# The first mixer of a two-layer decoder trunk, put in another order: keys first, one substitution for four groups, output projection in parts

## The chip, the cores and the metric

The kernel runs on one core of one Trainium2 chip. The metric is the time that the device takes for one execution of the whole program, in microseconds. Three runs of the kernel before took 2907.27, 2908.19 and 2913.11 us; their median, 2908.19 us, is the time that the change is compared with. The changed kernel computes the same function of the same inputs.

## The reference

The program is a trunk of two layers over 256 tokens of width 2048, in float32. Layer 0 mixes tokens with a gated DeltaNet, layer 1 with a sparse attention; each layer then has a normalization, a gated feed-forward part (5120 wide), another normalization and a gated addition. Only the mixer of layer 0 and the projection behind it are touched:

```python
def gdn_mixer(x, w_in, conv_w, a_log, dt_bias, norm_g, w_o):
    proj = x @ w_in                                   # 2048 x 12352
    qkv, z, a, b = ...
    qkv = silu(causal_dwconv(qkv, conv_w))            # four taps
    q, k = l2norm(q) * 128 ** -0.5, l2norm(k)         # 16 heads of 128
    beta, g = sigmoid(b), -exp(a_log) * softplus(a + dt_bias)   # 32 heads
    o = gated_delta_rule(q, k, v, g, beta)            # v: 32 heads of 128
    o = o * rsqrt(mean(o * o) + eps) * norm_g * silu(z)
    return o @ w_o                                    # 4096 x 2048
...
x = layer_norm(DN_ALPHA * x + gdn_mixer(x, ...), ln1_g[0], ln1_b[0])
```

Inside the delta rule a unit lower triangular system is solved for every head and chunk of tokens: (I + L) u = rhs, where L holds products of keys, scaled by beta and by decays exp(gc_i - gc_j). The kernel works with two chunks of 128 tokens, not four of 64, which gives the same result.

## The kernel before

**Large products.** Every product with weights is done in pieces of 512 KB (128 x 1024 numbers). `weights()` loads a piece on SP's queue into `raw` (three buffers), ScalarE copies it to `hi` in a shorter format (L107), and VectorE writes the rest to `lo` (L108), three buffers each; both have the priority of instructions 1000 places earlier. TensorE then multiplies hi with both halves of x and lo with one. `gemm_t_steps` does it with the weights as the stationary side (8 matmuls of 512 columns and 8 of 256 for one piece, output in PSUM tiles `mm_ps`), `gemm_steps` with x as the stationary side (12 matmuls of 512 columns, or 24 of 256, output `b_ps`). Both draw their PSUM tiles from the same ring "mm" of four banks, two at a time.

**Groups.** The mixer treats the 16 key heads and 32 value heads in eight groups g of two key heads and four value heads. For a group it runs, in the order of the program:

- `values(g)`: v, 8 pieces with four tiles of 128 columns, each convolved by `conv` (`fold` copies half of the PSUM tile on ScalarE, L186, VectorE adds the other half into `pd`, L187, then `ac` and three taps, tanh and a product), transposed and scaled into `vt`
- `zgate(g)`: the gate z, 8 pieces
- `keys(g+1)`: k and q of the next group, 4 pieces each, convolved in the same way
- `inverses(g)`: GpSimd loads the inverses of the 32 x 32 diagonal blocks into `pm`, TensorE multiplies them with L (`w_ps`), ScalarE copies that into W
- `front(g+1)`: decays from the rows `grow` (loaded by SP into `qd`), sums of squares, the products of keys and queries (`g_ps`), L; then L goes to DRAM (`lt`) and comes back as `ld` in another layout, and GpSimd inverts the diagonal blocks by 31 steps of a multiplication (L505) and a subtraction (L507), eight columns wide, masks L, and sends the inverses to DRAM (`tt`)
- `solve(g)`: for both chunks a (0 and 1) the start y0 = pm rhs, then three times y = y0 - W y, the last of which is u; each step is four small matmuls into `s_ps` (L517) and a subtraction on VectorE (L567). Between the chunks `rhs` gets the part of u of chunk 0 (`vt`, L559), and y0 is copied on ScalarE (L562)
- `outputs(g)`: o for both chunks (`o_ps`), its squares on ScalarE (`sqs`, L582, a ring of its own), rsqrt on VectorE, the product with z (`ot`), a transposition and the split into `oT`.

**What sets the order.** The engines run their instructions in order. The order on each is decided by a scheduler when the program is built: among the instructions whose inputs and buffers are there by its own estimate, it takes the one that stands first in the program. A tile of a ring can be written when the earlier users of its buffer are through. So large products of later groups can be drawn in between the steps of a solve, as long as buffers for them are free.

**Behind the groups.** `oT` holds all 32 heads. `project()` multiplies them with w_o in five blocks of columns (three of 512, two of 256, 64 pieces), adds them to x, which is loaded a second time (L870), takes the statistics, and `layer_norm` follows.

The lines that matter most here:

```python
def fold(self, pool, out, ps):
    t = pool.tile([P, S], F32, tag="fold", name="fold", bufs=2)
    nc.scalar.activation(t[:m], ps[:, S:], AF.Copy)
    nc.vector.tensor_tensor(out, ps[:, :S], t[:m], op=ALU.add)
...
sq = pool.tile([P, P], F32, tag="sqs", name="sqs")
for h in h4:
    nc.scalar.activation(sq, ps[:, h], AF.Square, accum_out=...)
```

## Time and profile before

The profile is one execution, taken by the hardware profiler; times inside it count from the start of its span.

| | |
|---|---|
| median of three runs | 2908.19 us (2907.27 to 2913.11) |
| span of the profiled execution, which is also its time here | 2914.3 us |
| the mixer's groups (first large matmul to the last `oT`) | 12.8 to 869 us |
| its output projection (`b_ps<-hi,oT`) | 757.7 to 970 us |
| substitution on GpSimd (L505, L507) | 496 operations, 229.9 us busy |
| VectorE, first 970 us | 662.0 us busy |
| ScalarE, first 970 us | 454.3 us busy |
| TensorE, first 970 us | 903.7 us busy |

An engine's busy time is the time in which an instruction of it was running; a pause is printed in brackets with what ended it. TensorE is the engine with the least slack, so what counts is what it waits for and at which clock it runs (1.00 is full speed, 0.50 half). Other engines' pauses cost nothing as long as TensorE does not wait for them.

### The profile page before, as it was taken

What the parts mean: (1) busy time and instruction counts of PE and PEld (TensorE: products, weight loads), DVE (VectorE), ACT (ScalarE), POOL (GpSimd) and SP (SyncE); (2) the same over time, 40 slices, a digit from 0 to 9 for tenths busy, and PEclk for the clock granted to TensorE, in tenths of its full rate; (3) what the DMA queues carried; (4) which work ended last, traced back from release to release, by engine and by line L of the source; (5) the groups of instructions that cost most, each with busy time, mean ns of one, the idle gap of its engine ahead of it and who ended that gap; (6) DMA issues with size and microseconds to landing.
All of it is one profiled execution on the core that took longest, in us unless ns stands there. A gap on an engine that the chain in (4) does not pass through costs nothing.

```text
span 2914.3 us, 41870 instructions
## 1 busy us (share of the span) xinstructions
PE 2826.4 (97%) x15790; PEld 2458.8 (84%) x15790; DVE 1860.0 (64%) x3148; ACT 1399.7 (48%) x2147; POOL 399.3 (14%) x720
## 2 busy tenths in 40 slices
PE   8899999999899999999999999999999999999999
PEld 7677888788688888888888988888888888888887
DVE  6667876787455666666545575666566666654465
ACT  4444554455333555555433453455465555543344
POOL 0552445344400000000000000030000000000000
PEclk9999999999999999999999999999999999999999
DMA  7655555556456566667655566554556666665555
GB/s 196 165 127 136 158 157 154 150 150 164 119 184 205 160 200 201 205 201 206 195 194 195 173 200 196 169 178 145 184 168 195 195 189 195 196 194 193 190 181 188
DMA packets 425947, 520.94 MB, mean 179 GB/s; under 512 B 28268, under 2 KB 329712, under 8 KB 425488
## 3 DMA queue, kind: packets, MB, share of 16 engines
q1 hardware_dynamic: 418576, 499.91, 56.6%
q0 software_dynamic: 7168, 18.35, 2.6%
q8 instruction: 124, 2.03, 0.3%
q14 instruction: 79, 0.65, 0.1%
HBM read 513.94 MB, written 7.39 MB: 179 GB/s over the span
## 4 chain that ended last, share of the span: by engine, by line
PE 83%; DMA 7%; DVE 4%; POOL 2%; issue 2%; ACT 2%; SPq 0%; DVEq 0%; ACTq 0%; POOLq 0%
PE mm_ps L126 31%; PE mm_ps L130 16%; PE b_ps L150 10%; PE b_ps L154 10%; PE b_ps L151 10%; DMA raw<-in_gdn_w_in 2%; DVE lo L108 2%; PE s_ps L517 2%; POOL xt L505 1%; DMA qd<-grow 1%; POOL xi L507 1%; ACT hi L107 1%; DMA raw<-in_ple_w_gate 1%; DMA ld<-lt 1%; PE w_ps L517 1%
## 5 line engine op out<-in xcount | busy, mean ns | idle before, releaser
L108 DVE TENSOR_TENSOR lo<-raw,hi 128x1024 fp32r<-128x1024 f32 x925 | 1135.5, 1229 | 878.1 <-ACT hi L107 841.6
L107 ACT ACTIVATE hi<-raw 128x1024 fp32r<-128x1024 f32 x925 | 977.0, 1057 | 1268.5 <-PE b_ps L151 489.3
L126 PE MATMUL mm_ps<-xT,hi 128*128 128x512 f32 x4176 | 1072.1, 396 | 19.2 <-DVE pd L187 6.8
L126 PEld LDWEIGHTS mm_ps<-xT,hi 128*128 128x128 f32 x4176 | 752.2, 190 | 154.1 <-ACT hi L107 12.5
L130 PEld LDWEIGHTS mm_ps<-xT,lo 128*128 128x128 f32 x4176 | 578.5, 190 | 43.6
L130 PE MATMUL mm_ps<-xT,lo 128*128 128x256 f32 x4176 | 602.2, 284 | 0.0
L150 PE MATMUL b_ps<-hi,xT 128*128 128x512 f32 (+2 forms) x736 | 277.9, 385 | 9.9 <-ACT hi L107 8.9
L151 PE MATMUL b_ps<-hi,xT 128*128 128x512 f32 (+2 forms) x736 | 276.0, 381 | 0.0
L151 PE MATMUL b_ps<-hi,hTA 128*128 128x512 f32 (+1 forms) x640 | 212.2, 347 | 0.0
L150 PE MATMUL b_ps<-hi,hTA 128*128 128x512 f32 (+1 forms) x640 | 212.2, 347 | 0.0
L154 PE MATMUL b_ps<-lo,xT 128*128 128x512 f32 (+2 forms) x736 | 190.5, 380 | 1.5 <-DVE lo L108 1.5
L150 PEld LDWEIGHTS b_ps<-hi,xT 128*128 128x128 f32 x736 | 140.7, 191 | 37.4 <-ACT hi L107 11.5
L203 POOL DMA_DIRECT2D lng<-in_ln_g x16 | 9.4, 589 | 1145.3 <-DVE lo L108 560.8
L151 PEld LDWEIGHTS b_ps<-hi,xT 128*128 128x128 f32 x736 | 139.8, 190 | 24.0 <-DVE xT L291 0.3
L154 PEld LDWEIGHTS b_ps<-lo,xT 128*128 128x128 f32 x736 | 132.8, 190 | 26.6 <-DVE lo L108 1.9
L154 PE MATMUL b_ps<-lo,hTA 128*128 128x512 f32 (+1 forms) x640 | 138.6, 347 | 0.0
L151 PEld LDWEIGHTS b_ps<-hi,hTA 128*128 128x128 f32 x640 | 121.2, 189 | 15.0
L150 PEld LDWEIGHTS b_ps<-hi,hTA 128*128 128x128 f32 x640 | 121.2, 189 | 15.0
L505 POOL TENSOR_TENSOR xt<-ld,xi 128x60 f32<-128x60 f32 (+24 forms) x248 | 113.5, 458 | 89.7 <-DMA ld<-lt 70.9
L507 POOL TENSOR_TENSOR xi<-xi,xt 128x60 f32<-128x60 f32 (+24 forms) x248 | 116.4, 469 | 19.4
L154 PEld LDWEIGHTS b_ps<-lo,hTA 128*128 128x128 f32 x640 | 105.1, 189 | 15.0
L150 PE MATMUL b_ps<-hi,oT 128*128 128x512 f32 (+1 forms) x320 | 108.0, 353 | 0.6 <-DVE x L225 0.5
(260 smaller groups left out, 2637.0 us busy)
## 6 DMA issues: line engine op xcount, KB each, us to landing
raw<-in_gdn_w_in SPq DMA_DIRECT2D x193, 512.0 KB, 4.3
raw<-in_ffn_w_gate SPq DMA_DIRECT2D x160, 512.0 KB, 5.0
raw<-in_ffn_w_up SPq DMA_DIRECT2D x160, 512.0 KB, 4.7
raw<-in_ffn_w_down SPq DMA_DIRECT2D x160, 512.0 KB, 3.5
raw<-in_dsa_w_in SPq DMA_DIRECT2D x80, 512.0 KB, 3.6
raw<-in_gdn_w_o SPq DMA_DIRECT2D x64, 512.0 KB, 3.7
raw<-in_ple_w_gate SPq DMA_DIRECT2D x64, 512.0 KB, 3.9
raw<-in_dsa_w_o SPq DMA_DIRECT2D x32, 512.0 KB, 4.0
```

The lines of the kernel that those rows point to most:

```text
L107: nc.scalar.activation(hi, raw, AF.Copy)
L108: ins = nc.vector.tensor_tensor(lo, raw, hi.bitcast(F32), op=ALU.subtract)
L126: nc.tensor.matmul(q[:m, :], hi[:, k, o:o + m], x[:, k0 + k].rearrange("p a b -> p (a b)"), start=k0 + k == 0, stop=False)
L130: nc.tensor.matmul(q[:m, S:], lo[:, k, o:o + m], x[:, k0 + k, 0, :], start=False, stop=k0 + k == kt - 1)
L150: nc.tensor.matmul(ps[a][:, :n], xh, hi[:, k, :], start=k0 + k == 0, stop=False)
L151: nc.tensor.matmul(ps[a][:, :n], xl, hi[:, k, :], start=False, stop=False)
L154: self.last = nc.tensor.matmul(ps[a][:, :n], x(k0 + k)[:, 0, a * P:(a + 1) * P], lo[:, k, :], start=False, stop=k0 + k == kt - 1)
L203: ins = self.nc.gpsimd.dma_start(out=r, in_=bass.AP(tensor=src.tensor, offset=src.offset, ap=[[0, P], [1, n]]))
L505: nc.gpsimd.tensor_tensor(tmp[:, :m, :w], bcast(ld[:, i + 1:, i], m, 1), xi[:, :m, i:i + 1].to_broadcast([P, m, w]), op=ALU.mult)
L507: nc.gpsimd.tensor_tensor(xi[:, :m, i + 1:], xi[:, :m, i + 1:], tmp[:, :m, :w], op=ALU.subtract)
L517: nc.tensor.matmul(ps[:, h], lhs[:, h], rhs[:, h], start=first, stop=last)
```

## The change

- **Keys.** The keys of groups 0 to 3 are computed first, those of 4 to 7 behind the first group's values and gate. All eight stay in SBUF. Queries are computed group by group (`queries(g+1)`).
- **Substitution.** `lower(g)` makes L of a group and sends its diagonal blocks to DRAM on GpSimd's queue. `substitution()` loads those of four groups as `ld`, one 32 x 32 block on each of the 128 partitions, turns the blocks over into `lT`, and runs the 31 steps on VectorE: one multiplication and one subtraction each, over all columns done so far. It is a generator: `weights()` takes `share` steps out of it with every piece of weights, two for the first four groups and one for the second, and what is left is drained in one go (the line `self.go_(self.aside)`).
- **Masks and clamps.** The mask on L is multiplied in where W is written, now on VectorE, and the mask on q k^T on two products instead of four. The clamps of the decays go from VectorE to ScalarE (Relu with a bias), and `lower` and `front` both load the rows of `grow`.
- **Outputs.** Both chunks share one rsqrt of 8 columns. The scratch of the squares is a tile of the ring "fold". `oT` is a tile of one group, in a ring of two.
- **Projection in parts.** `mixed(g, n)` multiplies the heads of n groups with their rows of w_o in four blocks of 512 columns and adds the product to x, which stays where it was loaded first: two groups at a time, ahead of the solves of groups 2, 4 and 6, and group 6 alone behind the solve of group 7. `project()` has the four heads of group 7 left.

The first two fences are TensorE's order at the end of group 1's solve: `s_ps` are the steps of the solve, `o_ps` its output products, `mm_ps` large matmuls (of values of group 2). Before:

```order
L517 MATMUL s_ps<-y,W 128x128 x4
L126 MATMUL mm_ps<-xT,hi 128x512 x7
L130 MATMUL mm_ps<-xT,lo 128x256 x8
L126 MATMUL mm_ps<-xT,hi 128x512 x8
L130 MATMUL mm_ps<-xT,lo 128x256
L517 MATMUL s_ps<-y,W 128x128 x4
L579 MATMUL o_ps<-u,qd 128x128 x4
L130 MATMUL mm_ps<-xT,lo 128x256 x7
L126 MATMUL mm_ps<-xT,hi 128x512 x8
```

and of the change, where line numbers are its own:

```order
L504 MATMUL s_ps<-y,W 128x128 x4
L124 MATMUL mm_ps<-xT,hi 128x512 x3
L128 MATMUL mm_ps<-xT,lo 128x256 x8
L504 MATMUL s_ps<-y,W 128x128 x4
L504 MATMUL s_ps<-u,n_2186 128x128 x4
L504 MATMUL s_ps<-vt,pm 128x128 x4
L504 MATMUL s_ps<-y_2919,W 128x128 x4
L504 MATMUL s_ps<-y,W 128x128 x8
L608 MATMUL o_ps<-u,qd 128x128 x4
L607 MATMUL o_ps<-u,qo 128x128
L608 MATMUL o_ps<-u,qd 128x128
```

What moved: before, every step of the solve is followed by large matmuls; in the change the last six steps and the output products stand one behind the other, without a large matmul between them.

The second place is ScalarE's order around the squares of a group (`sqs`), with the `fold` of the convolutions that follow. Before, at group 3:

```order
L562 ACTIVATE y_4341<-s_ps 128x512
L540 ACTIVATE vt<-v_ps,sv 128x128 x8
L107 ACTIVATE hi<-raw 128x1024 x5
L582 ACTIVATE sqs,oss<-o_ps 128x128 x4
L107 ACTIVATE hi<-raw 128x1024 x2
L186 ACTIVATE fold<-mm_ps 128x256 x2
L402 ACTIVATE ac<-pd_110,cw 128x256
```

and in the change, at group 1:

```order
L590 ACTIVATE y_2919<-s_ps 128x512
L611 ACTIVATE sqs,oss<-o_ps 128x128 x5
L184 ACTIVATE fold<-mm_ps 128x256
L611 ACTIVATE sqs,oss<-o_ps 128x128 x3
L406 ACTIVATE ac<-pd_109,cw 128x256
L184 ACTIVATE fold<-mm_ps 128x256 x2
L468 ACTIVATE L<-qd,ngc 128x128 x8
```

What moved: the folds of the next group's values now stand behind the squares whose buffers they take over, the first one behind the four squares of chunk 0 (and one of chunk 1), the second behind those of chunk 1, and between y0 and the squares no `hi` is left. Behind them come the clamps of `lower`, eight in a row.

The third place is VectorE's order in the solve of group 3, where the substitution of the second four groups is drained (`xt` and `xi` are its two operations). Before, the steps y, y and u of chunk 1, at group 1:

```order
L567 TENSOR_TENSOR y<-y_2447,s_ps 128x512
L108 TENSOR_TENSOR lo<-raw,hi 128x1024 x2
L567 TENSOR_TENSOR y<-y_2447,s_ps 128x512
L108 TENSOR_TENSOR lo<-raw,hi 128x1024
L567 TENSOR_TENSOR u<-y_2447,s_ps 128x512
```

and in the change, the end of 33 operations of the substitution in a row:

```order
L497 TENSOR_TENSOR xi<-xi,xt 128x26x6
L495 TENSOR_TENSOR xt<-lT,xi 128x135
L497 TENSOR_TENSOR xi<-xi,xt 128x27x5
L495 TENSOR_TENSOR xt<-lT,xi 128x112
L497 TENSOR_TENSOR xi<-xi,xt 128x28x4
L495 TENSOR_TENSOR xt<-lT,xi 128x87
L497 TENSOR_TENSOR xi<-xi,xt 128x29x3
L495 TENSOR_TENSOR xt<-lT,xi 128x60
L497 TENSOR_TENSOR xi<-xi,xt 128x30x2
L495 TENSOR_TENSOR xt<-lT,xi 128x31
L595 TENSOR_TENSOR u<-y_4753,s_ps 128x512
```

What moved: the substitution, which stood on GpSimd, is on VectorE ahead of a step of the solve. The diff, cut to its core:

```diff
@@ weights()
+        for _ in range(self.share):
+            next(self.aside, None)
         return hi, lo
@@ residual()
-    def residual(self, xb, ps, st):
-        self.nc.vector.scalar_tensor_tensor(xb, xb, ALPHA, ps, op0=ALU.mult, op1=ALU.add)
-        self.nc.vector.bn_stats(st, xb)
+    def residual(self, xb, ps, st, scale=ALPHA):
+        if scale == 1.0:
+            self.nc.vector.tensor_tensor(xb, xb, ps, op=ALU.add)
+        else:
+            self.nc.vector.scalar_tensor_tensor(xb, xb, scale, ps, op0=ALU.mult, op1=ALU.add)
+        if st is not None:
+            self.nc.vector.bn_stats(st, xb)
@@ gdn_groups()
+        def lower(g, s):
+            i, k = g % 4, ks[g]
+            dm = rows_of(g)
+            L = Ls[g] = pool.tile([P, 2, 4, P], F32, tag="L", name="L", bufs=6)
...
+            for a in range(2):
+                for h in h4:
+                    nc.scalar.activation(L[:, a, h], dm[:, a, h], AF.Relu,
+                                         bias=self.ngc[:, a, 4 * g + h:4 * g + h + 1])
+                nc.scalar.activation(L[:, a], L[:, a], AF.Exp, scale=-1.0)
...
+            for b in range(4):
+                nc.gpsimd.dma_start(out=s["lt"][i, :, b].rearrange("q i j -> i q j"),
+                                    in_=L[32 * b:32 * b + 32, :, :, 32 * b:32 * b + 32].rearrange("p a h j -> p (a h) j"))
+
+        def substitution(s):
+            lt, tt = s["lt"], s["tt"]
+            ld = pool.tile([P, 32, 32], F32, tag="zs", name="ld")
+            nc.gpsimd.dma_start(out=ld, in_=lt.rearrange("g q b i j -> (g q b) i j"))
+            lT = pool.tile([P, 32, 32], F32, tag="u", name="lT")
+            nc.vector.tensor_copy(lT, ld.rearrange("p i j -> p j i"))
...
             for i in range(31):
-                w, m = 31 - i, i // 4 + 1
-                nc.gpsimd.tensor_tensor(tmp[:, :m, :w], bcast(ld[:, i + 1:, i], m, 1),
+                m, w = i + 1, 31 - i
+                tmp = pool.tile([P, 256], F32, tag="xt", name="xt")
+                tv = tmp[:, :m * w].rearrange("p (c j) -> p c j", c=m)
+                nc.vector.tensor_tensor(tv, bcast(lT[:, i, i + 1:], m, 1),
                                         xi[:, :m, i:i + 1].to_broadcast([P, m, w]), op=ALU.mult)
-                nc.gpsimd.tensor_tensor(xi[:, :m, i + 1:], xi[:, :m, i + 1:], tmp[:, :m, :w], op=ALU.subtract)
+                nc.vector.tensor_tensor(xi[:, :m, i + 1:], xi[:, :m, i + 1:], tv, op=ALU.subtract)
+                yield
@@ outputs()
-                sq = pool.tile([P, P], F32, tag="sqs", name="sqs")
+                sq = pool.tile([P, S], F32, tag="fold", name="sqs", bufs=2)[:, :P]
                 for h in h4:
                     nc.scalar.activation(sq, ps[:, h], AF.Square, accum_out=ss[:, a, h // 2, h % 2:h % 2 + 1])
...
+        def mixed(g, n):
+            scale = ALPHA if not g else 1.0
+            h = lambda k: self.heads[g + k // 4][:, k % 4]
+            for nb in range(4):
+                c = nb * 512
+                self.gemm(t["gdn_w_o"][4 * g * P:], c, 512, h, 4 * n,
+                          lambda a, ps: self.residual(self.x[:, a, c:c + 512], ps, None, scale))
...
+        b0 = scales(0)
+        for g in range(4):
+            lower(g, b0)
+        n = queries(0)
+        self.aside, self.share = substitution(b0), 2
+        f = front(0, n)
+        vt, zs = values(0, b0), zgate(0)
+        self.go_(self.aside)
+        self.share = 0
+        for g in range(4, 8):
+            self.go_(key_steps(g))
+        b1 = scales(1)
         for g in range(8):
-            s = n
-            values(s)
-            zgate(s)
-            if g < 7:
-                n = keys(g + 1)
-            inverses(s)
-            if g < 7:
-                front(n)
-            solve(s)
-            outputs(s)
+            s = b1 if g > 3 else b0
+            if g:
+                vt, zs = values(g, s), zgate(g)
+            n = queries(g + 1) if g < 7 else None
+            if g == 4:
+                self.go_(self.aside)
+                self.share = 0
+            inverses(g, s)
+            if g < 7:
+                e = front(g + 1, n)
+            if g in (2, 4, 6):
+                mixed(g - 2, 2)
+            u = solve(g, s, f, vt)
+            if g == 7:
+                mixed(6, 1)
+            outputs(g, f, u, zs)
+            f = e
+            if g == 1:
+                lower(4, b1)
+                lower(5, b1)
+            if g == 2:
+                lower(6, b1)
+                lower(7, b1)
+                self.aside, self.share = substitution(b1), 1
@@ run()
-        x = self.x = xp.tile([P, 2, D], F32, tag="x", name="x")
-        nc.sync.dma_start(out=x, in_=t["x"].rearrange("(a q) d -> q a d", q=P))
...
-            affine = self.project(pool, t["gdn_w_o"], lambda k: oT[:, k], 32, t["ln1_g"][0], t["ln1_b"][0],
-                                  lambda: self.prepare(0, pp), side=2)
+            affine = self.project(pool, t["gdn_w_o"][28 * P:], lambda k: last[:, k], 4, t["ln1_g"][0], t["ln1_b"][0],
+                                  lambda: self.prepare(0, pp), side=2, scale=1.0)
```

More of the change, by code (lines that the diff above doesn't have):

```diff
@@ L88, in __init__ @@
         self.behind = []
+        self.aside, self.share = iter(()), 0
+        self.xp = pool(name="xp", bufs=1, side="right")
+        self.x = self.xp.tile([P, 2, D], F32, tag="x", name="x")
     def after(self, ins, to, sync=False):
@@ L429, in keys @@
-        def keys(g):
-            s = {"g": g}
-            q = s["q"] = pool.tile([P, 2, S], F32, tag="q", name="q")
-            k = s["k"] = pool.tile([P, 2, S], F32, tag="k", name="k")
-            steps = (self.gemm_t_steps(w_in, 2048 + 256 * g, 256, self.xT, conv(16 + 2 * g, lambda n: k[:, n])),
-                     self.gemm_t_steps(w_in, 256 * g, 256, self.xT, conv(2 * g, lambda n: q[:, n])))
-            if not g:
-                for nb in range(4):
-                    load(nb)
-                    next(steps[0])
-                gates()
-            for x in steps:
-                self.go_(x)
-            return s
@@ L444, in sums @@
[L444 to L458 removed]
+        ks = {}
@@ new lines, in key_steps, with squares @@
+        def key_steps(g):
+            k = ks[g] = pool.tile([P, 2, S], F32, tag="k", name="k", bufs=8)
+            return self.gemm_t_steps(w_in, 2048 + 256 * g, 256, self.xT, conv(16 + 2 * g, lambda n: k[:, n]))
+        def squares(y, ps):
+            sq = pool.tile([P, 2, S], F32, tag="y0", name="sq")
+            nc.scalar.activation(sq, y, AF.Square)
+            for h in range(2):
+                for a in range(2):
+                    nc.tensor.matmul(ps[:, 2 * h + a:][:, 0:1], sq[:, h, a * P:(a + 1) * P],
+                                     self.ones[:, 0:1], start=True, stop=True)
@@ L459, in sums, with scales @@
+        def scales(b):
+            pss = self.sp.tile([P, 16], F32, tag="sp", name="kk_ps")
+            for i in range(4):
+                squares(ks[4 * b + i], pss[:, 4 * i:4 * i + 4])
+            ss, ik = small("kss", 16), small("kik", 16)
+            c, nc1, sv = small("c", 2, 8, 2), small("nc1", 16), small("sv", 2, 8, 2)
             nc.vector.tensor_scalar(ss, pss, 4 * RMS_EPS, None, op0=ALU.add)
-            rk = self.rsqrt(pool, ss[:, 0:4], 4)
+            rk = self.rsqrt(pool, ss, 16)
@@ L515, in mul, with inverses @@
+                yield
+            nc.gpsimd.dma_start(out=tt.rearrange("g q b c j -> (g q b) c j"), in_=xi)
+        def mul(lhs, rhs, ps=None):
             ps = ps if ps is not None else self.sp.tile([P, 4, P], F32, tag="bk", name="s_ps")
             for h in h4:
-                nc.tensor.matmul(ps[:, h], lhs[:, h], rhs[:, h], start=first, stop=last)
+                nc.tensor.matmul(ps[:, h], lhs[:, h], rhs[:, h], start=True, stop=True)
             return ps
-        def inverses(s):
+        def inverses(g, s):
@@ L618, in project @@
-    def project(self, pool, src, h, kt, g, b, prepare, side=1):
+        def mixed(g, n):
[5 more added lines that the diff above has]
+                          lambda a, ps: self.residual(self.x[:, a, c:c + 512], ps, None, scale))
+        first = [key_steps(g) for g in (0, 1)]
+        for nb in range(4):
+            load(nb)
+            for x in first:
+                next(x)
@@ L619, in project @@
+    def project(self, pool, src, h, kt, g, b, prepare, side=1, scale=ALPHA):
         blocks = ((0, 512), (512, 512), (1024, 512), (1536, 256), (1792, 256))
```

234 lines of the change are left out of this document (114 added, 120 removed).

## The prediction

> **What bounds the kernel now.** The page comes first. TensorE is busy for 97% of the span, and the change touches only the first mixer, so the question is where TensorE stands still or runs slowly there, and whether the new order makes that less or more.
>
> ```profile
> span 2914.3 us, 41870 instructions
> PE 2826.4 (97%) x15790; PEld 2458.8 (84%) x15790; DVE 1860.0 (64%) x3148; ACT 1399.7 (48%) x2147; POOL 399.3 (14%) x720
> ```
>
> The busy time by stretches of the mixer is the second view. The columns are the stretch, its length, the busy time of PE, its weight loads, DVE, ACT and POOL (with counts), the granted clock, the DMA share and GB/s. Group 0 is begun before 150 us, the last group's solve falls after 750 us, and the output projection ends near 970 us.
>
> ```profile
> 50.00:150.00 100.00, 83.50 (x448) 71.45 (x447) 68.78 (x141) 45.16 (x78) 42.84 (x76) 0.94 0.62 165
> 150.00:750.00 600.00, 570.90 (x3316) 497.29 (x3316) 454.14 (x1039) 303.30 (x575) 258.14 (x472) 0.98 0.56 150
> 750.00:800.00 50.00, 41.38 (x202) 35.09 (x201) 23.47 (x52) 17.76 (x39) 24.16 (x52) 0.86 0.35 104
> 800.00:970.00 170.00, 169.40 (x969) 148.23 (x968) 89.73 (x122) 65.71 (x77) 5.36 (x12) 1.00 0.60 193
> ```
>
> From 50 to 150 us TensorE idles 16.5 us, over the 600 us of the steady groups 29.1 us, from 750 to 800 us 8.6 us, and then hardly at all. That is all the idle time that a better order can give back, some 54 us, with the slow clock that follows long pauses (0.94, 0.98 and 0.86). The timeline of TensorE names the two large pauses of the first group and shows what a pause costs afterwards.
>
> ```profile
> 106.48 3.66 PE L126 MATMUL mm_ps<-xT,hi 128*128 128x512 f32 x8 [5.73 <-ACT hi L107]
> 109.98 1.11 PE L130 MATMUL mm_ps<-xT,lo 128*128 128x256 f32 x8
> 110.93 2.00 PE L126 MATMUL mm_ps<-xT,hi 128*128 128x512 f32 x8
> 148.68 1.57 PE L517 MATMUL w_ps<-pm,L 128*128 128x96 f32 x6 [9.29 <-DMA pm<-tt]
> ```
>
> The first 8 matmuls after the pause of 5.73 us take 109.98 - 106.48 = 3.5 us, the next 8 (110.93 on) 2.00: 1.5 us are lost to the slow clock. The 9.29 us are the wait for the inverses that GpSimd works out one group at a time.
>
> **What the change takes away.** (1) The two pauses of group 0, 15.0 us, and about 4.5 us of slow clock behind them (1.5 as above, twice that for the longer pause): 19.5 us. Their cause goes, since the substitution of four groups now has the matmuls of keys 4 to 7, 16 pieces of weights, as cover. (2) The pauses from 750 to 800 us: 8.6 us, and 4.4 for the clock, which is 0.14 below full over 50 us but partly in the pauses themselves: 13 us. (3) Of the 29.1 us of the steady groups about half, 14.5, since some end on weights that queue on SP behind the transfers of L and ld (these move to GpSimd's queue), others on the convolution, which stays; with half of the clock loss (0.02 of 600 us) 6 us: 20 us. (4) In the projection 14 pieces of 256 columns become pieces of 512. The starts of the lo matmuls that close two successive pieces of 512 columns tell what one takes:
>
> ```profile
> 1501.88 1.07 PE L154 MATMUL b_ps<-lo,hTA 128*128 128x512 f32 x4
> 1504.60 1.07 PE L154 MATMUL b_ps<-lo,hTA 128*128 128x512 f32 x4
> 1600.06 1.12 PE L154 MATMUL b_ps<-lo,hTA 128*128 128x256 f32 x8
> 1602.93 1.12 PE L154 MATMUL b_ps<-lo,hTA 128*128 128x256 f32 x8
> ```
>
> 2.72 against 2.87 us, so 14 x 0.15 = 2.1 us. Sum taken away: 54.6 us; 36 if the steady pauses all stay, 76 if they all go with their clock loss (41 in place of 20).
>
> **What it adds: seven open tails.** The order shows the price. In outputs() the scratch of the squares is now taken from the ring "fold" of two buffers, out of which every convolution's first step also draws. So the folds of values(g+1) wait for the squares of group g, the four PSUM tiles of the large matmuls stay full, and TensorE has nothing to put between the last steps of solve(g): in the rows above, s_ps, s_ps, s_ps, o_ps stand one behind the other, where before some twenty large matmuls stood between two steps. The length of a step is read where VectorE was waiting for it (timeline of all engines):
>
> ```profile
> 840.52 1.05 PE L517 MATMUL s_ps<-y,W 128*128 128x128 f32 x8
> 841.41 1.06 PE L579 MATMUL o_ps<-u,qd 128*128 128x128 f32 x8
> 841.62 0.69 DVE L567 TENSOR_TENSOR u<-y,s_ps 128x512 f32<-128x512 f32 x1 [1.30 <-PE s_ps L517]
> 842.51 0.28 ACT L582 ACTIVATE sqs<-o_ps 128x128 f32<-128x128 f32 x1 [0.73 <-PE o_ps L579]
> 842.91 0.28 ACT L582 ACTIVATE sqs<-o_ps 128x128 f32<-128x128 f32 x1
> ```
>
> VectorE begins 1.10 us after the step's first matmul (841.62 - 840.52) and needs 0.69. How soon TensorE follows, a place shows where it waited for vt:
>
> ```profile
> 651.12 1.11 DVE L559 SCALAR_TENSOR_TENSOR vt<-s_ps,nc,vt 128x128 f32<-128x128 f32 x4
> 651.52 0.75 PE L517 MATMUL s_ps<-vt,pm 128*128 128x128 f32 x4 [0.61 <-DVE vt L559]
> ```
>
> The first of the four vt (336 ns, below) ends at 651.46, and TensorE starts 0.06 later. A step is 1.85 us. TensorE is taken for 0.81 of it (a little less than 841.41 - 840.52), so each step leaves 1.04 us idle. The rest of the tail comes from the groups by line:
>
> ```profile
> L559 DVE SCALAR_TENSOR_TENSOR vt<-s_ps,nc,vt 128x128 f32<-128x128 f32 x32 | 8.9, 336 | 0.0
> L562 ACT ACTIVATE y<-s_ps 128x512 f32<-128x512 f32 x16 | 9.4, 587 | 4.1 <-PE s_ps L517 3.7 <-PE ss_ps L453 0.4
> L186 ACT ACTIVATE fold<-mm_ps 128x256 f32<-128x256 f32 x64 | 20.8, 373 | 1.1 <-PE mm_ps L130 0.7
> L187 DVE TENSOR_TENSOR pd<-mm_ps,fold 128x256 f32<-128x256 f32 x64 | 24.1, 413 | 0.0
> L402 ACT ACTIVATE ac<-pd,cw 128x256 f32<-128x256 f32 x64 | 29.4, 501 | 21.2 <-DVE pd L187 20.6
> ```
>
> In groups 0, 1, 3 and 5, which have no projection in between: four steps that end in y or u, 4.2 us; the step through vt, which TensorE follows head by head, 1.2; y0 on ScalarE (0.59, and the drain of its matmuls) 0.9. Then the 12 output matmuls of the two halves take about 2.5 us (24 records at 0.1), while five squares at 0.40 (842.91 - 842.51) from 1.10 on end at 3.1, a fold (0.37) and its add (0.41) at 3.95: 1.45 idle. Two large matmuls later the second bank is wanted, which waits for three squares, ac (0.50), fold and add: 2.5 less 0.45, 2.0. Sum 9.75 us. In groups 2, 4 and 6 the projection of two groups fills the first half and three steps stay open: 3.1 + 0.3 + 3.45 = 6.9. Together 4 x 9.75 + 3 x 6.9 = 60 us; 45 if each hand-over costs nothing.
>
> In a tail TensorE works about 45% of the time. What the clock makes of that is read at a like place:
>
> ```profile
> 238.12 1.11 PE L477 MATMUL g_ps<-k 128*128 128x256 f32 x4
> 240.88 0.30 PE L592 MATMUL ot_ps<-ident,ot 128*128 128x128 f32 x1 [1.65 <-DVE ot L588]
> 242.18 0.84 PE L592 MATMUL ot_ps<-ident,ot 128*128 128x128 f32 x3 [1.00 <-DVE ot L588]
> 242.91 1.92 PE L517 MATMUL w_ps<-pm,L 128*128 128x96 f32 x8
> 250.60 1.03 PE L517 MATMUL w_ps<-pm,L 128*128 128x96 f32 x8
> 238.00:244.00 6.00, 3.35 (x17) 2.45 (x16) 5.56 (x15) 3.91 (x10) 0.00 (x0) 0.92 0.52 144
> 244.00:246.00 2.00, 2.00 (x8) 1.71 (x8) 2.00 (x5) 1.51 (x4) 0.00 (x0) 0.50 0.53 184
> 374.00:380.00 6.00, 3.38 (x19) 2.31 (x17) 6.00 (x14) 3.20 (x6) 5.06 (x13) 1.00 0.31 87
> 380.00:382.00 2.00, 1.96 (x11) 1.50 (x10) 2.00 (x3) 2.00 (x7) 1.84 (x3) 1.00 0.82 208
> ```
>
> Pauses of 1.65 and 1.00 us, with TensorE busy 3.35 of 6 us, were enough for the same 8 matmuls to take 1.92 us in place of 1.03, with 0.50 of the clock granted; a stretch as thin at 374 us (3.38 of 6) kept the full clock. A tail at half clock throughout its second half would lose about 5 us, with 1.7 us on the large matmuls behind it nearly 7, one untouched nothing. The two places tie, so I take 2.5 for each tail, 17.5 us, and keep 0 and 49 as ends. The Trainium skill, "TensorE: Matmul & The Clock Gate" (section "Why this matters for your kernels"), advises pauses of no more than about 3 us if the clock is to hold; by that rule the 17.5 would be 0 and the sum smaller by as much. The trace agrees at 374 us and not at 244, where pauses of at most 1.65 us stood ahead of a clock of 0.50.
>
> **Three smaller terms.** The substitution on VectorE is 31 steps of two operations for four groups. A 128x256 add takes 0.413 us (L187) and, from the next row, a 128x512 one 0.681, so 1.05 ns an element and 0.145 fixed.
>
> ```profile
> L567 DVE TENSOR_TENSOR y<-y,s_ps 128x512 f32<-128x512 f32 x32 | 21.8, 681 | 11.6 <-PE s_ps L517 11.6
> L505 POOL TENSOR_TENSOR xt<-ld,xi 128x60 f32<-128x60 f32 (+24 forms) x248 | 113.5, 458 | 89.7 <-DMA ld<-lt 70.9
> L247 DVE TENSOR_TENSOR rt<-rs 128x4 f32<-128x4 f32 x72 | 13.2, 184 | 1.4
> L419 ACT ACTIVATE qo<-qd,go 128x128 f32<-128x128 f32 x32 | 10.3, 391 | 22.1 <-DMA qd<-grow 22.1
> ```
>
> A set has 2 x 5456 elements (the sum over the steps of columns done by columns left): 11.4 + 62 x 0.145 = 20.4 us, two sets 41 us, against 230 us in 496 operations (L505 and its twin) on GpSimd, which nothing but group 0 and the last group waited for. VectorE was busy 454 of 600 us, so there is room, except at one place: the rest of the second set is drained ahead of group 4, and in VectorE's order 33 of its operations with some 6190 elements stand between y and u of group 3, without a lo among them. That is 6.5 + 4.8 = 11.3 us in front of a step that TensorE waits for; less what the step has already been charged, 9.5 us. Second, group 7: its solve is covered by the projection of group 6 up to u of the first half, but vt, y0, three steps, the squares, twelve small operations of rsqrt (0.18 each, L247), ot and oT stand ahead of the last projection: 1.2 + 0.9 + 3.1, then about 7 after the output matmuls, and 3 for the clock: 15 us (9 to 20). Third, ScalarE gets the clamps that VectorE did: 128 activations at about 0.39 (L419 is the like form), 50 us, of which lower() and front() put some 20 in a row ahead of hi in three places. The three pieces of weights that are split ahead cover about 8 us; I charge 6 us (0 to 25).
>
> The other moves I cost at nothing: masks on VectorE (16 adds of 256 and 16 of 384 elements), the smaller rsqrt count, 32 more adds into x at 0.68, since VectorE's sum stays within 10 us of what it was; x is loaded once, not twice (2 MB less), and the rows of grow twice (4 MB more). Without that slack these would show as TensorE waiting for lo.
>
> **Sum.** Added: 60 + 17.5 + 9.5 + 15 + 6 = 108; taken away 55; net +53. The profiled span of 2914.3 lies 6.1 above the median of the three runs, so 2914.3 + 53 - 6.1 = 2961 us. Low end: added 45 + 0 + 8 + 9 + 0 = 62, taken away 76: 2894. High end: 60 + 49 + 11 + 20 + 25 = 165, taken away 36: 3037.
>
> **Rivals.** (A) Faster: the wait for the inverses and SP's crowded queue were the real cost, and the tails are cheap. With 76 taken away and 8 + 9 added for the drain and group 7, the seven tails must cost less than 59 us, 8.4 each, to come out ahead; at 45 the time is 2894. For it: the 9.29 and 5.73 us pauses are real and do go. Against it: the step of 1.85 us is measured, and the order leaves no large matmul in the tails. (B) The clock stays whole, because no single pause in a tail is much longer than 2 us: 2961 - 17.5 = 2943. The row at 380 us is for it, the row at 244 us against it. (C) The clock falls to half in every tail: 2961 + 31.5 = 2992; the same two rows, the other way round. B is also what the Trainium skill's rule on pauses gives. (D) The bursts on ScalarE and VectorE are not covered, so that TensorE waits for hi and lo after each tail as well: 2961 + 19 = 2980, and with C 3011.
>
> **How the numbers follow.** Something near the forecast, tails at 60 with some of the clock, 0.45; B 0.15; C and D together 0.23; A 0.12, ending below 2902; the rest, 0.05, lands within 0.2% of the time before (about what a measurement of this kernel can tell from no change). So slower 0.83, same 0.05, faster 0.12. The range runs from A's side to C with D, 2898 to 3020.
>
> **What would show it.** In the profile of the changed kernel each of groups 0 to 6 should show TensorE waiting for VectorE's y and u, some 1 us each, four or three times, with a granted clock under 0.9 there, and a wait of the first z matmuls for pd; the wait of w_ps for pm and the pauses from 100 to 150 us should be gone; group 3 should have one pause of about 10 us. I am wrong if the tails together idle under 45 us, or if a large matmul stands between their steps.

## The result, and the profile after

The changed kernel takes 2934.22 us (median of 5 runs, 2921.75 to 2939.18), the kernel before, timed beside it, 2909.56 us (2907.27 to 2913.49). The ratio is 1.0075 with a 95% interval of 1.0056 to 1.0094: slower by 22 us by the ratio, 18.1 by the profiled spans. The forecast was 2961, slower by 53 us; the direction and the range hold, the size is more than twice too large.

The page, as for the kernel before:

```profile
span 2932.4 us, 40943 instructions
PE 2835.6 (97%) x15654; PEld 2462.2 (84%) x15654; DVE 1854.8 (63%) x3007; ACT 1426.5 (49%) x2259; POOL 115.3 (4%) x192
```

GpSimd gave up 284 us of work and VectorE is no busier, yet the span is 18.1 us longer. The busy time by stretches (length, PE, weight loads, DVE, ACT, POOL, granted clock, DMA share, GB/s) shows where; the mixer now ends at 992.9 us, where the first transposition of the normalization starts, before at 976.1:

```profile
50.00:150.00 100.00, 94.91 (x525) 82.00 (x524) 80.09 (x188) 69.11 (x148) 11.54 (x20) 0.97 0.68 190
150.00:500.00 350.00, 333.55 (x1880) 288.63 (x1880) 237.65 (x463) 178.69 (x350) 20.71 (x36) 0.99 0.54 155
500.00:600.00 100.00, 77.63 (x416) 67.73 (x415) 72.17 (x160) 41.08 (x86) 2.91 (x5) 0.85 0.39 122
600.00:900.00 300.00, 288.76 (x1577) 248.87 (x1576) 186.67 (x309) 138.95 (x248) 6.92 (x12) 0.99 0.51 153
900.00:992.90 92.90, 84.48 (x437) 71.69 (x436) 62.12 (x124) 35.28 (x59) 5.31 (x12) 0.93 0.41 134
```

The first group's pauses went (95 of 100 us busy, 83.5 before). One stretch stands out: 500 to 600 us, 22 us idle at a clock of 0.85. What TensorE waited for from 150 to 900 us, by the view of waits (instruction, what it waited for, us in all, times, longest), is a list of the tails and little else:

```profile
PE s_ps L504 <- DVE u L595: 17.8, 4, 14.3
PE s_ps L504 <- DVE y L595: 11.4, 14, 0.9
PE b_ps L148 <- DVE pd L185: 8.3, 7, 1.2
PE mm_ps L124 <- DVE pd L185: 4.1, 1, 4.1
PE s_ps L504 <- ACT y L590: 3.5, 7, 0.7
PE s_ps L504 <- DVE vt L587: 1.8, 4, 0.4
```

Without the one wait of 14.3 us for u, the waits of the seven tails add up to 3.5 + 11.4 + 8.3 + 3.5 + 1.8 = 28.5 us idle. The same view of the kernel before, 150 to 800 us, names quite other things:

```profile
PE ot_ps L592 <- DVE ot L588: 10.5, 5, 4.6
PE b_ps L150 <- ACT hi L107: 8.3, 4, 3.3
PE mm_ps L126 <- DVE pd L187: 6.8, 3, 3.0
PE v_ps L538 <- DVE v L407: 6.4, 5, 2.7
PE s_ps L517 <- DVE vt L559: 3.5, 3, 1.8
```

One tail in full, TensorE's timeline of the changed kernel at the end of group 1 (start, length, matmuls, and in brackets the idle time before and what ended it):

```profile
320.15 1.05 PE L504 MATMUL s_ps<-y,W 128*128 128x128 f32 x8
322.37 1.16 PE L504 MATMUL s_ps<-u,n 128*128 128x128 f32 x8 [1.16 <-DVE u L595]
323.97 1.26 PE L504 MATMUL s_ps<-vt,pm 128*128 128x128 f32 x8 [0.45 <-DVE vt L587]
325.92 1.16 PE L504 MATMUL s_ps<-y,W 128*128 128x128 f32 x8 [0.69 <-ACT y L590]
327.93 1.16 PE L504 MATMUL s_ps<-y,W 128*128 128x128 f32 x8 [0.85 <-DVE y L595]
329.87 1.64 PE L504 MATMUL s_ps<-y,W 128*128 128x128 f32 x8 [0.78 <-DVE y L595]
331.30 1.91 PE L608 MATMUL o_ps<-u,qd 128*128 128x128 f32 x8
333.00 0.63 PE L607 MATMUL o_ps<-u,qo 128*128 128x128 f32 x2
...
334.95 0.39 PE L608 MATMUL o_ps<-u,qd 128*128 128x128 f32 x2
336.52 0.50 PE L148 MATMUL b_ps<-hi,xT 128*128 128x512 f32 x1 [1.19 <-DVE pd L185]
```

From 320.15 to 336.52 are 16.37 us for 72 small matmuls, which follow each other every 0.111 us where nothing delays them: 8.0. So the tail costs 8.4 us (8.5 with the first gate matmul, as the table has it). Counted in this way (starts of rows, less 0.111 us for a small matmul, 0.119 for one of 256 columns, 0.227 for one of 512), all of the mixer gives this account of lost time:

| lost time, us | before | after |
|---|---|---|
| to 50 us | 10.8 | 12.3 |
| 50 to 150 us | 20.9 | 5.2, and 4.6 in one wait ahead of the first gate matmul |
| tails of groups 0 to 6 | | 9.7, 8.5, 4.3, 10.8, 4.3, 8.2, 4.3 = 50.1 |
| wait for u in group 3 | | 14.6 |
| end of group 7 | in the next row | 14.9 |
| all else (before: to 750, to 800, to 976 us) | 52.7 + 14.5 + 2.7 = 69.9 | 17.7 |
| sum to the normalization | 101.6 | 119.4 |

### The profile page after: what moved, and what is told of

It reads as the page before. It is cut to its first block, busy times and chain, and to the rows that moved or that the text cites. A ratio compares the mean times of both kernels' runs of the same rounds, so it can differ in the third digit from the quotient of the medians.

```text
span 2932.4 us, 40943 instructions
## 1 busy us (share of the span) xinstructions
PE 2835.6 (97%) x15654; PEld 2462.2 (84%) x15654; DVE 1854.8 (63%) x3007; ACT 1426.5 (49%) x2259; POOL 115.3 (4%) x192
## 4 chain that ended last, share of the span: by engine, by line
PE 91%; issue 3%; ACT 2%; DVE 2%; DMA 1%; POOL 0%; DVEq 0%; SPq 0%; ACTq 0%; POOLq 0%
PE mm_ps L124 31%; PE mm_ps L128 16%; PE b_ps L148 13%; PE b_ps L149 13%; PE b_ps L152 12%; PE s_ps L504 3%; PE o_ps L608 1%; ACT hi L103 1%; DMA qd<-grow 1%; DVE lo L104 0%; PE w_ps L504 0%; DVE y L595 0%; PE lg_ps L910 0%; PE sc_ps L860 0%; PE ot_ps L624 0%
## 5 line engine op out<-in xcount | busy, mean ns | idle before, releaser
L124 PE MATMUL mm_ps<-xT,hi 128*128 128x512 f32 (+1 forms) x4176 | 1068.2, 396 | 15.2 <-DVE mv L235 4.6
L124 PEld LDWEIGHTS mm_ps<-xT,hi 128*128 128x128 f32 (+1 forms) x4176 | 752.2, 190 | 150.2 <-ACT hi L103 9.2
L128 PEld LDWEIGHTS mm_ps<-xT,lo 128*128 128x128 f32 (+1 forms) x4176 | 575.2, 191 | 43.9 <-DVE lo L104 1.9
L128 PE MATMUL mm_ps<-xT,lo 128*128 128x256 f32 (+1 forms) x4176 | 596.4, 284 | 1.2 <-DVE lo L104 1.2
L148 PEld LDWEIGHTS b_ps<-hi,hTA 128*128 128x128 f32 x640 | 121.2, 189 | 14.9
L149 PE MATMUL b_ps<-hi,oT 128*128 128x512 f32 (+1 forms) x264 | 101.8, 388 | 0.0
L148 PE MATMUL b_ps<-hi,oT 128*128 128x512 f32 (+1 forms) x264 | 101.1, 386 | 0.0
L408 DVE SCALAR_TENSOR_TENSOR ac<-pd,cw,ac 128x256 f32<-128x256 f32 x192 | 87.0, 480 | 16.2 <-ACT ac L406 16.1
L184 ACT ACTIVATE fold<-mm_ps 128x256 f32<-128x256 f32 x261 | 84.4, 372 | 0.1
```

Of the source, the lines that this page charges most:

```text
L124: nc.tensor.matmul(q[:m, :], hi[:, k, o:o + m], x[:, k0 + k].rearrange("p a b -> p (a b)"), start=k0 + k == 0, stop=False)
L128: nc.tensor.matmul(q[:m, S:], lo[:, k, o:o + m], x[:, k0 + k, 0, :], start=False, stop=k0 + k == kt - 1)
L148: nc.tensor.matmul(ps[a][:, :n], xh, hi[:, k, :], start=k0 + k == 0, stop=False)
L149: nc.tensor.matmul(ps[a][:, :n], xl, hi[:, k, :], start=False, stop=False)
L408: nc.vector.scalar_tensor_tensor(ac, pd[:, k:k + S], w[:, k:k + 1], ac, op0=ALU.mult, op1=ALU.add)
```

## The experiments

Every kernel was timed beside the kernel before; the ratio is its time over that, with the 95% interval. Gains are differences of medians; by the ratios they come out 1 to 3 us apart where two kernels did not run together.

### The two shared buffers

The first four runs ask what the tails and the wait for u are worth. `own_squares` differs from the changed kernel in one line (of the scratch nothing is read, only the sums that come with it):

```diff
-                sq = pool.tile([P, S], F32, tag="fold", name="sqs", bufs=2)[:, :P]
+                sq = pool.tile([P, P], mybir.dt.bfloat16, tag="sqs", name="sqs")
```

> The changed kernel with one edit: the scratch of the squares in outputs() has a buffer of its own (128 bf16 values a partition) in place of one of the two of the ring fold. Theory (the shared ring leaves TensorE without large matmuls between the last steps of each solve): the open steps of groups 0, 1, 2, 4, 5 and 6, which took 9.1, 8.0, 4.0, 4.0, 7.9 and 4.0 us more than their matmuls need in the profile of the changed kernel, go, 37 us; the wait of 14.3 us in group 3 is covered by large matmuls, but one tail stays open behind it. Span 2932 - 37 - 14 = 2881 us, and 4 to 6 us large matmuls stand between the steps; TensorE waits for y and u of groups 0 to 2 and 4 to 6 less than 3 us in all. Rival (the cover is only borrowed, so the same time is lost later as waits for weights or for lo, since VectorE and ScalarE set the pace): within 10 us of 2932.

2919.26 us (2918.08 to 2922.24), ratio 1.0034 [1.0022, 1.0046]: 15 us won, not 50. The open steps of groups 0 to 2 and 4 to 6 are gone, as the theory had it, but new waits stand elsewhere, as the rival had it. Its waits, 150 to 920 us (the two for y and the one for u are those of group 3):

```profile
PE ot_ps L624 <- DVE ot L620: 14.9, 5, 4.5
PE s_ps L504 <- DVE u L595: 4.9, 1, 4.9
PE s_ps L504 <- DVE y L595: 1.6, 2, 0.9
```

`lt_in_ring_L` leaves the scratch and moves the other buffer (`len(Ls) > 4` is true for the second set):

```diff
-            lT = pool.tile([P, 32, 32], F32, tag="u", name="lT")
+            lT = pool.tile([P, 32, 32], F32, tag="L" if len(Ls) > 4 else "u", name="lT", bufs=6 if len(Ls) > 4 else 1)
```

> The changed kernel with one edit: the transposed copy lT of the second set of four groups is taken from the ring of L (six buffers) in place of the single buffer that it shares with u. Theory (u of group 3 cannot be written before the last step of the substitution has read lT, so the whole rest of the set stands ahead of it): the wait of 14.3 us for u in group 3 falls to about 1.2, with some 3 us of slow clock behind it: span 2932 - 16 = 2916 us. Rival (the drain written ahead of group 4 sets the burst, as the prediction had it): the burst stays in one piece, before or behind u, and the span stays at 2932 or moves by less than 5 us.

2918.52 us (2907.14 to 2926.99), 1.0024 [1.0012, 1.0036]: 16 us less, as expected. In its timeline the wait for u in group 3 is that of any other tail:

```profile
533.35 1.16 PE L504 MATMUL s_ps<-y,W 128*128 128x128 f32 x8
535.82 1.16 PE L504 MATMUL s_ps<-u,n 128*128 128x128 f32 x8 [1.31 <-DVE u L595]
```

In VectorE's order the substitution's steps now stand behind u as well. So the drain ahead of group 4, which is still there, did not hold u back. lT lay in the only buffer of u, and u could be written when the last multiplication had read lT. VectorE's timeline of the changed kernel shows it to the instruction: u stands behind the last operation that reads lT, and ahead of the last subtraction, which doesn't:

```profile
549.67 0.21 DVE L495 TENSOR_TENSOR xt<-lT,xi 128x31 f32<-128x31 f32 x1
549.99 0.69 DVE L595 TENSOR_TENSOR u<-y,s_ps 128x512 f32<-128x512 f32 x1
550.59 0.20 DVE L497 TENSOR_TENSOR xi<-xi,xt 128x31 f32<-128x31 f32 x1
```

`both_rings` has both edits.

> Both edits together (own scratch for the squares, lT of the second set from the ring of L). Theory: all seven tails and the wait in group 3 go: 2932 - 37 - 10 - 16 = 2869 us, faster than the kernel before by some 40 us; the end of group 7 (14 us of idle time and clock) stays. Rival (cover borrowed): 2905 or more.

2902.15 us (2899.40 to 2905.12), 0.9975 [0.9965, 0.9985]: 32 us less than the changed kernel, where 63 were expected, and 7 to 8 us less than the kernel before. So the two shared buffers decide the sign of the whole change. No tail is left, and the view of waits, 150 to 900 us, shows what came in their place:

```profile
PE ot_ps L624 <- DVE ot L620: 12.0, 4, 4.1
PE b_ps L148 <- ACT hi L103: 4.2, 1, 4.2
PE v_ps L563 <- DVE L L472: 2.6, 1, 2.6
PE b_ps L148 <- ACT oT L626: 2.2, 3, 0.8
```

`before_shared` puts the scratch of the old order into the ring fold (the reverse of the first diff, in the kernel before).

> The kernel before with one edit: the scratch of the squares comes from the ring fold, as in the changed kernel. Theory (the shared ring alone opens the tails, in the old order too): groups 0 to 6 lose about 8 us each, 7 x 8 = 56: span 2914 + 56 = 2970 us. Rival (the tails belong to the new order, which has fewer large matmuls left per group): 2914 to 2920.

2978.90 us (2977.04 to 2984.57), 1.0240 [1.0226, 1.0253]: 69 us, more than the 56 expected. Its waits, 150 to 830 us:

```profile
PE ot_ps L592 <- DVE ot L588: 33.6, 8, 4.8
PE s_ps L517 <- DVE y L567: 15.7, 20, 0.9
PE b_ps L150 <- DVE pd L187: 8.3, 7, 1.2
PE s_ps L517 <- DVE u L567: 5.8, 7, 1.2
PE s_ps L517 <- ACT y L562: 4.8, 7, 0.7
```

Each step loses what it loses in the new order, over seven tails of full length (no projection covers a part of three of them): 37.7 us in all against 28.5. And the waits for ot go from 10.5 to 33.6 us: here chunk 0's ot stands in the tail too, with nothing to cover it (4.76 us at 396 us, between the steps and the first gate matmul). The same one-line edit thus costs 69 us in one order and 15 in the other.

### What takes the place of the tails

Four edits on top of both_rings look for what holds the rest. `rows_by_gpsimd`:

```diff
-            nc.sync.dma_start(out=dm, in_=bass.AP(tensor=self.grow.tensor, offset=self.grow.offset + 4 * g * P,
+            nc.gpsimd.dma_start(out=dm, in_=bass.AP(tensor=self.grow.tensor, offset=self.grow.offset + 4 * g * P,
```

> both_rings with one more edit: the rows of grow (qd<-grow, 24 transfers of 512 KB) are issued on GpSimd's queue in place of SP's. Theory (part of the cover that the two rings give back is lost to SP's queue: a qd row waits there for one of two qd buffers, 6.8 us at 359 us in both_rings, with the weights behind it): the wait of 4.2 us for hi at 378 us and the clock behind it go, and some of the 5.3 us at 488 to 495 us; 2900 - 7 = 2893 us by the span. Rival (the waits come from the bursts of clamps on ScalarE, not from the queue): 2900, within 3.

2893.55 us (2892.19 to 2899.41), 0.9950 [0.9937, 0.9963]: 7 to 9 us less, near the 7 expected, but by luck, since it took away another wait than the one named: that for hi is still 3.5 us long (at 373 us), while this one of both_rings, ahead of the first gate matmul, is gone:

```profile
119.00 0.77 PE L148 MATMUL b_ps<-hi,xT 128*128 128x512 f32 x1 [4.41 <-ACT qd L531]
```

From 50 to 150 us TensorE is now never short:

```profile
50.00:150.00 100.00, 99.59 (x571) 86.95 (x570) 83.08 (x190) 71.36 (x150) 15.98 (x26) 1.00 0.72 201
```

The clamps on ScalarE are all still there, so that wait came from the rows on SP's queue (16 transfers in the trace, not 24) and not from the clamps. `late_turn` takes the transposes of ot out of outputs() and writes them later:

```diff
                 vt, zs = values(g, s), zgate(g)
+                turn(*o)
...
-            outputs(g, f, u, zs)
+            o = outputs(g, f, u, zs)
```

> both_rings with one more edit: the transposes of ot and the split into oT are written behind values and zgate of the next group in place of directly behind the outputs. Theory (with the tails filled, the large matmuls that covered the chain squares, rsqrt, ot are used up ahead of it, so TensorE now waits for ot: 4.3, 2.0, 2.7 and 3.7 us in groups 1, 3, 5 and 6, with 6 us of oT waits and clock behind them): some 15 us go, span 2900 - 15 = 2885. Rival (the amount of large matmuls is what lacks, so that another wait takes the place): 2895 or more.

2905.64 us (2896.94 to 2907.86), 0.9981 [0.9972, 0.9991]: nothing won. The rival holds: w_ps then waits for the PSUM tile that ot must read first (3.3 us), and others for vt.

> both_rings with the edits of rows_by_gpsimd and late_turn together. Theory (two separate causes): 2900 - 7 - 15 = 2878 us by the span. Rival (the waits share one cause, too few large matmuls): no better than the better of the two alone.

`rows_and_turn` has both edits: 2890.04 us (2887.01 to 2891.65), 0.9932 [0.9919, 0.9944], 12 us less than both_rings; beside the rows the late transposes bring 3.5 us by the medians, 5 by the ratios, not 15. `set_on_gpsimd` gives the 31 steps of both_rings back to GpSimd, still for four groups at once (`nc.vector` to `nc.gpsimd` in the two lines of the loop).

> both_rings with the substitution of four groups on GpSimd in place of VectorE, so that only the engine of the change is undone. A step of the kernel before took GpSimd 0.46 us for 44 elements on the mean, mostly fixed, so a set of 62 takes between 28 us (all fixed) and 114 (all by the element). Theory (the order, all keys first, is what hides the inverses, the engine matters little): the first set still ends inside the matmuls of keys 4 to 7, some 45 us, and the span is 2900 within 6 us, with VectorE's busy time down by some 43 us. Rival (the set needs VectorE's speed): TensorE waits for pm at group 0 for 15 to 60 us, 2915 to 2960.

2892.75 us (2890.61 to 2893.88), 0.9941 [0.9927, 0.9955]: 9 us less, so the slower engine is the better one. The groups by line show GpSimd at 839 and 767 ns an operation, 100 us in all for what VectorE did in 42:

```profile
L495 POOL TENSOR_TENSOR xt<-lT,xi 128x31 f32<-128x31 f32 (+15 forms) x62 | 52.0, 839 | 19.6 <-DVE lT L485 14.9
L497 POOL TENSOR_TENSOR xi<-xi,xt 128x31 f32<-128x31 f32 (+15 forms) x62 | 47.6, 767 | 4.9
```

No wait for pm is left all the same. What hides the inverses is that keys come first; the engine only decides whose queue the set stands in. `three_edits_more` is rows_and_turn with the set on GpSimd.

> both_rings with the three edits rows on GpSimd's queue, late transposes and substitution on GpSimd. rows_and_turn measured 2890.0 and set_on_gpsimd 2892.8 against 2902.2 of both_rings. Theory (VectorE's late work and the crowded queue are separate costs): 2902 - 12 - 9 = 2881 us. Rival (both edits remove the same waits): 2888 to 2892.

2899.16 us (2895.32 to 2901.30), 0.9955 [0.9942, 0.9967]: 9 us worse than rows_and_turn (7 by the ratios), which neither theory had; against set_on_gpsimd it is 6 us by the medians and 4 by the ratios, whose intervals overlap. One wait accounts for the loss against rows_and_turn:

```profile
197.59 1.11 PE L128 MATMUL mm_ps<-xT,lo 128*128 128x256 f32 x8
203.03 1.14 PE L504 MATMUL w_ps<-pm,L 128*128 128x96 f32 x4 [4.34 <-DMA pm<-tt]
```

With the matmuls at half speed behind it, 8.0 us are lost between 150 and 250 us, against 0.3 in rows_and_turn; the mixer ends 8.7 us later. Rows and set together on GpSimd make the inverses late; that the rows' transfers hold up the set there is likely, and was not tested by itself. On top of it `more_for_group_7` keeps one group's projection back for the last solve:

```diff
-                mixed(g - 2, 2)
+                mixed(g - 2, 1 if g == 6 else 2)
...
-                mixed(6, 1)
+                mixed(5, 2)
```

> three_edits_more with one more edit: the projection of head group 5 is kept back, so that the solve of group 7 has two groups' projection behind it (about 43 us of large matmuls) in place of one (22 us), and solve 6 one in place of two. Theory (the open steps at the end of group 7 are a lack of large matmuls there): the waits for vt, y0 and two y (1.8, 1.1, 2.0, 2.0 us with their clock) go, the wait of 4.5 us for ot and 1.2 us of clock stay: 6 to 8 us less than three_edits_more. Rival (solve 6 loses what group 7 gains): no difference beyond 2 us.

2887.78 us (2884.20 to 2890.58), 0.9914 [0.9902, 0.9927]: 11 us less, a little more than expected.

### Parts of the change by themselves

`rsqrt_by_half` is both_rings with the rsqrt of before:

```diff
-            r = self.rsqrt(pool, z.rearrange("p a j r -> p (a j r)"), 8)
-            for a, ps in enumerate(pss):
+                r = self.rsqrt(pool, z[:, a].rearrange("p j r -> p (j r)"), 4)
```

> both_rings with one part of the change undone: each half of outputs() has its own rsqrt of 4 again, in place of one of 8 for both, so that ot of the first half need not wait for the squares of the second. Theory (the common rsqrt puts the squares of the second half ahead of the first ot): the waits for ot in groups 1, 3, 5, 6 and 7 (4.1, 1.9, 2.5, 3.5 and 4.5 us) shrink by 1 to 2 us each, 2902 - 7 = 2895 by the median. Rival (twelve more small operations of 0.2 us a group stand in VectorE's queue, and lo comes later): 2902 to 2908.

2886.88 us (2885.72 to 2887.70), 0.9913 [0.9900, 0.9926]: 15 us less (18 by the ratios), twice what was expected, and the largest single gain on both_rings. Its waits, 150 to 890 us, beside those of both_rings above:

```profile
PE ot_ps L620 <- DVE ot L616: 5.2, 4, 1.6
PE b_ps L148 <- DVE pd L185: 3.3, 2, 2.0
PE b_ps L148 <- ACT hi L103: 2.5, 1, 2.5
```

The waits for ot fall from 12.0 to 5.2 us, because ot of chunk 0 no longer stands behind the squares of chunk 1; that is 7 of the 15 us, and the rest is spread over smaller waits and the clock and was not split up. Does this cost belong to the changed kernel as it is? `changed_rsqrt_half` makes the edit there alone.

> The changed kernel with one edit: an rsqrt of 4 for each half of outputs() in place of one of 8, the edit that brought 15 us to both_rings. Theory (in the changed kernel the open tails leave large matmuls behind them that cover the chain to ot, so the common rsqrt costs there only what group 7 shows, and the two costs hide each other): 0 to 5 us less than 2934, so 2929 to 2934 by the median. Rival (the common rsqrt costs the same 15 us in every order, apart from the tails): 2919.

2927.88 us (2923.80 to 2933.18), 1.0062 [1.0046, 1.0078]: 6 us less by the medians, 4 by the ratios, whose intervals overlap, and far from 15. So the two costs largely hide each other: as long as the tails are open, large matmuls are left over behind them, and these cover the chain to ot. `before_lt_gpsimd` makes one move of the change in the old order:

```diff
-                nc.sync.dma_start(out=lt[:, b].rearrange("q i j -> i q j"),
+                nc.gpsimd.dma_start(out=lt[:, b].rearrange("q i j -> i q j"),
...
-            nc.sync.dma_start(out=ld, in_=bass.AP(tensor=lt.tensor, offset=lt.offset, ap=[[0, 4], [1024, 32], [1, 1024]]))
+            nc.gpsimd.dma_start(out=ld, in_=bass.AP(tensor=lt.tensor, offset=lt.offset, ap=[[0, 4], [1024, 32], [1, 1024]]))
```

> The kernel before with one part of the change alone: the transfers of L (lt) and ld are issued on GpSimd's queue in place of SP's. Theory (about half of the pauses in the steady groups of the kernel before end on weights that queue on SP behind lt and ld): the waits for hi of 3.3, 2.1 and 2.7 us and some of those for pd and v go: 2910 - 10 = 2900 us. Rival (the weights are late because raw and lo run behind, not because of these transfers, or GpSimd's own queue delays the inverses by as much): 2907 to 2915.

2897.95 us (2895.27 to 2903.02), 0.9955 [0.9941, 0.9969]: 14 us less by the medians, 13 by the ratio. In its waits from 50 to 780 us that for hi is down from 8.3 to 0.7 us and that for v from 6.4 to 0.4, and the pause of 5.73 us in group 0 is gone; the waits for the inverses grew from 9.3 to 19.6 us in all, 12.9 of them in group 0:

```profile
PE w_ps L517 <- DMA pm<-tt: 19.6, 4, 12.9
PE b_ps L150 <- ACT hi L107: 0.7, 2, 0.4
PE v_ps L538 <- DVE v L407: 0.4, 1, 0.4
```

### Versions that beat both kernels

> rsqrt_by_half with the rows of grow on GpSimd's queue and more projection kept back for group 7. Theory (three separate causes: chain to ot, SP's queue, cover at the end; measured alone as 15, 9 and 11 us): 2887 - 9 - 8 = 2870 us. Rival (they share waits, as three_edits_more did): 2882 or more.

2879.43 us (2878.77 to 2881.70), 0.9897 [0.9880, 0.9913]: the best of all, 30 us under the kernel before and 55 under the change. It keeps the substitution on VectorE. Against rsqrt_by_half 5 to 7 us came of the 17 expected, so its causes share waits too.

> rsqrt_by_half with the substitution on GpSimd and more projection kept back for group 7; the rows of grow stay on SP's queue, since the two shared GpSimd in three_edits_more. Theory: 2887 - 9 - 8 = 2870 us. Rival (VectorE's relief is the same as that of the shorter chain): 2880 or more.

2884.81 us (2882.80 to 2886.11), 0.9912 [0.9899, 0.9926]: 2 us under rsqrt_by_half, so here the rival holds: once the chain to ot is short, the relief of VectorE and the cover for group 7 together bring nothing more that these runs can tell.

## Why the prediction was right in direction and wrong in size

**Taken away, forecast 55.** The pauses of group 0: 20.9 us of lost time before, 5.2 after beside the new wait: 15.7 of the 19.5 forecast. Their cause was only half as told: in before_lt_gpsimd, which keeps the old substitution, the pause of 5.73 us is gone too, so that one came from SP's queue and not from the inverses. The steady groups and the stretch from 750 to 800 us: 69.9 before, 17.7 after, so 52 us where the prediction charged 13 + 20 = 33. This is one of the two places where it went wrong: it let half of the steady pauses stay. before_lt_gpsimd shows SP's queue, the reason that step (3) gave, to be worth 13 to 14 us in the old order. But the 52 us are no gain of their own: both_rings, which has no tails, loses 50.2 us from 150 to 900 us and 15.6 from there to the normalization, 65.8 where the kernel before loses 69.9. These are in part new waits, of moves that the prediction put at nothing: undoing the common rsqrt wins 15 us there, and taking the rows of grow off SP's queue 7 to 9. In the changed kernel the rsqrt is worth 4 to 6, so there the large matmuls that the tails left over cover most of it; for the other waits that is an inference, which no run shows by itself. The 2.1 us for wider pieces of the projection were not measured either.

**The open tails, forecast 60 and 17.5 for the clock.** The mechanism was right: own_squares and before_shared, one line each, take the tails away and bring them about. The step was right too: 1.05 and 1.12 us lost in the rows at 327.93 and 325.92, forecast 1.04. The sum over a tail was mis-sized, and this is the step that failed. In group 1 the rows give, beside 1.7 us of clock (0.90 granted over 17 us), 3.5 for three steps (4.2 for four in the forecast: the fourth is covered by the output products of chunk 0), 0.7 for vt (1.2), 1.1 for y0 (0.9), 1.4 for the first gate tile (1.45) and nothing for the second bank (2.0), where a fold ahead of the tail had freed one. That is 6.7, not 9.75; in groups 2, 4 and 6 it is 4.3, not 6.9. Over seven tails the second bank alone is 14 us and the fourth step 7. The sign of being wrong that the prediction named, tails that idle under 45 us together, is there: 28.5 us by the view of waits.

**The clock.** The windows of the tails give 0.81, 0.90, 1.00, 0.56, 1.00, 0.90 and 1.00 for groups 0 to 6. Times their lengths (18, 17, 10, 18, 11, 17, 10 us) that is 3.4 + 1.7 + 7.9 + 1.7 = 14.7 us against 17.5: near in sum, though more than half of it stands in group 3, behind the long wait.

```profile
320.00:337.00 17.00, 11.89 (x77) 10.70 (x76) 5.60 (x11) 4.08 (x20) 2.30 (x4) 0.90 0.24 71
450.00:460.00 10.00, 7.90 (x61) 7.00 (x60) 3.45 (x5) 3.21 (x12) 2.30 (x4) 1.00 0.41 120
550.00:568.00 18.00, 14.08 (x64) 12.72 (x64) 4.15 (x10) 2.46 (x12) 2.91 (x5) 0.56 0.11 37
```

The rule that the prediction quoted from the Trainium skill ("TensorE: Matmul & The Clock Gate", section "Why this matters for your kernels": pauses of no more than about 3 us) therefore holds in groups 2, 4 and 6, where no pause was over 1.19 us and the clock stayed at 1.00, and doesn't in groups 0, 1 and 5, where none was longer but there were six of them in place of four, and 0.81, 0.90 and 0.90 were granted. The 14.32 us in group 3 and the 0.56 behind them agree with it.

**The drain, 9.5.** 14.6 us (1.3 of it the step itself, which the prediction had charged to the tails), and for another reason than given: not the drain ahead of group 4 but the buffer that lT shares with u. The operations ahead of u took 13 us where 11.3 were forecast: the largest start 0.46 us apart, and each takes 0.42. **Group 7, 15.** 14.9. **The bursts on ScalarE, 6.** One wait of 4.6 us was there, but rows_by_gpsimd, where it is gone, shows that the rows on SP's queue caused it; the clamps cost nothing that can be seen in that stretch. The substitution on VectorE was to take 41 us and took 42.0.

**The sum.** Tails 25 too high, clock 3 too high, steady pauses 19 too low, group 0 4 too high, the wait for u 5 too low: 53 - 25 - 3 - 19 + 4 + 5 = 15, where the mixer ends 16.8 us later and the span is 18.1 longer. (A slip in the working: with all steady pauses left, 54.6 less 20 is 34.6 us taken away, not 36, so the high end should be 1 us higher.) The deeper fault is that the terms were added as if each stood alone. Tails and steady pauses draw on the same stock of large matmuls: what stands idle in one place is cover at the next.

**The rivals.** B's 2943 us lies nearer to the measured 2934 than the forecast does, but by luck: B has the clock whole, and it lost 14.7 us. A's condition held, since the tails cost 7.2 us each, clock included, where A asked for less than 8.4; yet the kernel is not faster, because the wait for u and group 7 took 29.5 us and not A's 17, and the relief was 68 us and not 76. D's waits for hi and lo behind the tails did not come: 1.2 us for lo and none for hi from 150 to 900 us.

## What to carry to other kernels

A scratch tile put into another tile's ring is not free memory: ask which instructions wait for that buffer, and what TensorE would have done meanwhile; the same line cost 15 us in one order and 69 in the other. On an engine that is busy 97% of the time, closing a pause gives back only what the next thing in line doesn't take: 15 of the 51 us expected of own_squares, until the chain behind them was shortened as well. So sum a reordering by its stock of cover, stage by stage, and not by single pauses.
